# A two-layer trunk with RWKV-7 mixing: triangular blocks inverted by substitution on VectorE for all heads at once, and the chunk chains of two feature tiles taken together

## The chip, the cores and the metric

The kernel runs on one core of one Trainium2 chip. The metric is the device time of one execution in microseconds, as the median of several runs. Times in the trace are microseconds from the first instruction of one profiled execution. PE is TensorE, DVE is VectorE, ACT is ScalarE, POOL is GpSimd and SP is SyncE, which issues most DMAs.

## The reference

One sequence of 256 tokens with 2048 features goes through two layers. Layer 0 mixes tokens by sparse attention with an indexer, layer 1 by RWKV-7; each is followed by a squared-ReLU MLP. The change touches only the scan of layer 1 and the products made for it:

```python
def step(state, inp):
    r_t, k_t, v_t, w_t, kk_t, a_t = inp
    sa = jnp.einsum('bhij,bhj->bhi', state, -kk_t)
    state = (state * w_t[:, :, None, :] + sa[..., None] * (kk_t * a_t)[:, :, None, :]
             + v_t[..., None] * k_t[:, :, None, :])
    return state, jnp.einsum('bhij,bhj->bhi', state, r_t)
_, o = lax.scan(step, state0, (seq_first(rh), seq_first(kh), seq_first(vh),
                               seq_first(dh), seq_first(kk), seq_first(ah)))
```

There are 32 heads of 64 features. The kernel takes the scan in chunks of 64 tokens. Inside a chunk the values that the state is updated with solve a unit triangular system of 64 unknowns, so each chunk of each head needs the inverse of a 64x64 unit triangular matrix: 32 heads x 4 chunks = 128 such systems.

## The kernel before

Activations lie with features on the partitions: 16 feature tiles of 128 features (two heads each) by 256 tokens. Weights come from HBM as pieces of 128x512 (`raw`, six buffers), and each is split into a high part `whi` by ScalarE (L92) and a low part `wlo` by VectorE or, for the pieces named in the phase's `g`, by GpSimd (L94). A dense unit is 16 columns of three matmuls (L184 to L186) of 256 tokens, 48 in all. The phases are `dsa`, `mlp0`, `project`, `scan` and `mlp1`. A planner orders each engine's instructions from the order in the program, priorities (`high_priority(URGENT)` puts work forward) and its own costs of instructions; it also places the semaphore waits.

In `project`, `elements(f)` makes for each tile f the operands of the chunks, `ar` and `bk`, and writes them to HBM (`hd`). Value weights belong to `scan`, but the value of tile 0 is made at the end of `project`.

In `scan`, `prepare(f)` loads the operands of a tile, makes its value (`value`, one dense unit) and the masked products `at` of `bk` and `ar` (L921, L922), transposes `bk` and the value, and makes `akv`. `inverse(f)` inverts the systems of a tile. It takes 32x32 diagonal blocks, begins with their pairs of rows, and doubles the size of what is inverted in four levels; a level is 16 matmuls of 32x32 at L977, a predicated copy on VectorE (L979), 16 matmuls at L984, a transpose on VectorE (L986) and a copy on ScalarE (L989). Then two blocks are merged into one of 64 (L997, L1004). `chain(f)` goes through the four chunks: the state's part (L1032), a sum on VectorE (L1034), the inverse applied (L1037), a copy by ScalarE (L1038), the output (L1040, copied at L1042) and the new state (L1049, L1051, L1058). `finish(f)` normalises and gates the result. When tiles 3, 7, 11, 13 and 15 are done, the output projection `b_w_o` of their block is put in a list in groups, and from tile 5 on one group is taken per tile. The loop over f emits `chain(f)` and `inverse(f+2)` at high priority, then `prepare(f+3)` and `finish(f)`. The phase `scan` has 23 buffers of 128x512 (`A`) and 13 of 128x256 (`B`).

Of the kernel before, what the change touches and what calls it, by code (L numbers as in the profile page):

```python
# [43 lines left out]
AHEAD, AHEAD_INV = 3, 2  # L44
# [19 lines left out]
for _n, _w in (("ident", 128), ("blockones", 128), ("headcol", 2), ("ones", 2), ("mask_a", 256),  # L64
               ("reset", 256), ("pair", 32), ("lvl", 128), ("i32", 32), ("half", 4)):
    CST[_n] = (_at, _w)
    _at += _w
# [34 lines left out]
class Trunk:  # L102
# [587 lines left out]
    def rwkv_project(s, keep):  # L690
# [28 lines left out]
        s.hd = [[s.dram.tile([P, 512], F32, name=f"hd{i}_{f}") for i in range(3)] for f in range(NF)]  # L719
        cols = [k * P for k in range(16)]  # L720
# [52 lines left out]
    def rwkv_scan(s):  # L773
        todo, om, pre = [], [], []
        for f in range(AHEAD):
            pre.append(s.prepare(f))
            if not f:
                s.pairs()
            if f < AHEAD_INV:
                s.inverse(f, pre[f])  # L780
        for f in range(NF):
            cur = pre.pop(0)
            with s.tc.high_priority(URGENT):
                s.chain(f, cur)
            if f + AHEAD_INV < NF:
                with s.tc.high_priority(URGENT):
                    s.inverse(f + AHEAD_INV, pre[AHEAD_INV - 1])
            if f + AHEAD < NF:
                pre.append(s.prepare(f + AHEAD))
            om.append(s.finish(f, cur))  # L790
            if todo and f >= LATE:
                todo.pop(0)()
            if f in CUTS:
                todo += [lambda b=f // 4, o=om, g=g, n=f % 4 + 1 - len(om): s.out_group("b_w_o", 1, b, g, o, n)
                         for g in range(4)]
                om = []
        for t in todo:
            t()

    def pairs(s):  # L800

        nc = s.nc
        i32 = s.cv("i32").unsqueeze(1).to_broadcast([P, 4, 32])
        s.z1, s.yl, s.zf, s.sbd, s.at_sbd = [], [], [], [], 0
        for i in range(3):
            z = s.tp.tile([P, P], F32, name=f"sbd{i}")
            nc.vector.memset(z, 0.0)
            s.sbd.append(z)
        for i in range(2):
            z = s.tp.tile([P, 4, 32], F32, name=f"z1_{i}")  # L810
            nc.scalar.copy(z, i32)
            s.z1.append(z)
            ys = []
            for l in range(4):
                y = s.tp.tile([P, 4, 32], F32, name=f"y{l}_{i}")
                nc.scalar.copy(y, i32)
                ys.append(y)
            s.yl.append(ys)
        for i in range(4):
            z = s.tp.tile([P, 4, 64], F32, name=f"zf_{i}")  # L820
            nc.vector.memset(z, 0.0)
            s.zf.append(z)

# [72 lines left out]

    def value(s, f, v):
        w = s.wload(s.io["b_w_v"][f])
        s.nc.scalar.copy(v, s.dense(w, s.xv, [i * P for i in range(16)]))
        return v  # L900

    def prepare(s, f):
# [13 lines left out]
        for h in range(2):  # L916
            hs = slice(h * 64, h * 64 + 64)
            p = s.bank("m")
            for c in range(4):
                cc = slice(c * P, c * P + P)  # L920
                mm(p[:, cc], bk[hs, cc], ar[hs, cc], start=True, stop=True)  # L921
            nc.vector.tensor_tensor(at[h].rearrange("p (c q) x->p c q x", c=2),  # L922
                                    p.rearrange("p (c q x)->p c q x", c=2, q=2), mask, op=OP.mult)
# [9 lines left out]
        uv = s.A().rearrange("p (c x)->p c x", c=4)  # L933
# [13 lines left out]
        akv = s.B()  # L947
        nc.scalar.copy(akv, p[:, :S])
        return dict(ar=ar, bkt=bkt, uv=uv, at=at, g=g, bv=bv, akv=akv)

    def inverse(s, f, d):
# [4 lines left out]
        at, i = d["at"], f % 2  # L956
        rows = [slice(32 * q, 32 * q + 32) for q in range(4)]
        nt = lambda q, u, c0: at[u // 2][rows[q], 2 * (u % 2) + (1 if q < 2 else 0), c0:c0 + 32]
        z1 = s.z1[i]
        pair = s.cv("pair").bitcast(U32)  # L960
        for q in range(4):
            for h in range(2):
                src = at[h][rows[q]].rearrange("p (c e) x->p c e x", e=2)[:, :, 1 if q < 2 else 0, 32 * q:32 * q + 32]
                nc.vector.copy_predicated(z1[rows[q], 2 * h:2 * h + 2, :],
                                          pair[rows[q]].unsqueeze(1).to_broadcast([32, 2, 32]), src)
        blk = lambda t, q, u: t[rows[q], u * 32:(u + 1) * 32]
        flat = lambda t: t.rearrange("p u x->p (u x)")
        tile = lambda: s.tp.tile([P, P], F32, name=f"xz{i}", bufs=4)
        z, x = flat(z1), tile()
        nc.vector.transpose(x, z)  # L970
        zf = s.zf[f % 4]
        for l in range(4):
            y = s.yl[i][l]
            p = s.bank("ij"[i])
            for u in range(4):
                for q in range(4):
                    mm(blk(p, q, u), nt(q, u, 32 * q), blk(x, q, u), start=True, stop=True)  # L977
            lvl = s.cv("lvl")[:, l * 32:(l + 1) * 32].bitcast(U32).unsqueeze(1).to_broadcast([P, 4, 32])
            nc.vector.copy_predicated(y, lvl, p[:, :P].rearrange("p (u x)->p u x", u=4))  # L979
            y = flat(y)  # L980
            p = s.bank("ij"[i])
            for u in range(4):
                for q in range(4):
                    mm(blk(p, q, u), blk(y, q, u), blk(z, q, u), start=True, stop=True)  # L984
            x = tile()
            nc.vector.transpose(x, p[:, :P])  # L986
            if l < 3:
                z = tile()
                nc.scalar.copy(z, p[:, :P])  # L989
        for q in range(4):  # L990
            o = 32 * (q % 2)
            (nc.scalar.copy if q % 2 else nc.vector.tensor_copy)(zf[rows[q], :, o:o + 32], p[rows[q], :P].rearrange("p (u x)->p u x", u=4))

        p = s.bank("ij"[i])
# [3 lines left out]
        yo = tile()  # L998
        for q in (1, 3):
            nc.scalar.copy(yo[rows[q]], p[rows[q], :P])  # L1000
        p = s.bank("ij"[i])
# [7 lines left out]
    def behind(s, ins, prev):  # L1009
# [3 lines left out]
                            reason="sums in one bank")  # L1013

    def chain(s, f, d):

        nc = s.nc
        ar, bkt, uv, at, zf, akv = (d[k] for k in ("ar", "bkt", "uv", "at", "zf", "akv"))
        mm = nc.tensor.matmul
        d["o"] = ot = s.tp.tile([P, S], F32, name="ot", bufs=2)  # L1020
        st = None
        hs = [slice(0, 64), slice(64, 128)]
        for c in range(4):
# [4 lines left out]
            p = s.bank("ab"[f % 2])  # L1028
            if st is None:
                rs = akv[:, g]  # L1030
            else:
                mm(p[:, :P], ar[:, cc], st, start=True, stop=True)  # L1032
                rs = s.tp.tile([P, P], F32, name="rs", bufs=2)
                nc.vector.tensor_tensor(rs[pu], p[pu, :P], akv[pu, g], op=OP.add)  # L1034
            pd, pn = p[:, P:2 * P], p[:, 2 * P:3 * P]
            for h in range(2):
                mm(pd[pu, hs[h]], zf[pu, 2 * h + c // 2, :], rs[pu, hs[h]], start=True, stop=True)  # L1037
            nc.scalar.copy(uv[pu, c, :], pd[pu])  # L1038
            for h in range(2):
                last = mm(p[pv, hs[h]], at[h][:, c, xr:xr + 64], uv[:, c, hs[h]], start=st is None, stop=True,  # L1040
                          skip_group_check=st is not None)
            nc.scalar.copy(ot[pv, g], p[pv, :P])  # L1042
            if c < 3:
                pc = s.pc[:, f, c:c + 1]
                new = s.sbd[s.at_sbd % 3]
                s.at_sbd += 1
                if st is not None:
                    dec = s.tp.tile([P, P], F32, name="sd", bufs=2)
                    nc.vector.tensor_scalar(dec, st, pc, None, op0=OP.mult)  # L1049
                for h in range(2):  # L1050
                    s.behind(mm(pn[hs[h], hs[h]], bkt[:, c * P + h * 64:c * P + h * 64 + 64], uv[:, c, hs[h]],  # L1051
                                start=True, stop=True), last)
                for h in range(2):
                    o, i, k = new[hs[h], hs[h]], pn[hs[h], hs[h]], pc[hs[h]]
                    if st is None:
                        nc.vector.tensor_scalar(o, i, k, None, op0=OP.mult)
                    else:
                        nc.vector.scalar_tensor_tensor(o, i, k, dec[hs[h], hs[h]], op0=OP.mult, op1=OP.add)  # L1058
                st = new

    def finish(s, f, d):
# [4 lines left out]
        B = lambda: s.tp.tile([P, S], F32, name="fin", bufs=FIN)  # L1066
# [18 lines left out]
        return s.split(w, t=s.O() if f // 4 % 2 else s.tp.tile([P, 512], F32R, name="om", bufs=OM))  # L1085
# [12 lines left out]
def build(tc, io):  # L1098
    with ExitStack() as ctx:
# [27 lines left out]
def constants():  # L1127
# [13 lines left out]
    c["pair"][:] = (j % 2 == 1) & (i == j - 1)  # L1141
    for l, b in enumerate((2, 4, 8, 16)):
        c["lvl"][:, l * 32:(l + 1) * 32] = ((i // b) % 2 == 1) & (j // b == i // b - 1)
# [109 lines left out]
```

## Time and profile before

| | |
|---|---|
| time, median of 3 runs | 2794.97 us (2776.96 to 2795.97) |
| the profiled execution | 2790.62 us |
| its span, first to last instruction | 2788.7 us |
| mean granted TensorE clock | 0.963 |
| instructions | 64443 |
| PE, DVE, ACT, POOL busy | 94%, 70%, 47%, 48% of the span |

The rest of the text counts times in the span. Busy shares are means over stages with different limits; matmuls are pipelined and their ends are modelled, so a busy PE is not PE at its peak.

### The profile page before, as it was taken

How to read it: one execution, taken by the hardware profiler on the slowest of the kernel's cores; microseconds unless marked ns; L12 is line 12 of the kernel's file. 1: busy time of each engine (PE TensorE's matmuls, PEld its weight loads, DVE VectorE, ACT ScalarE, POOL GpSimd, SP SyncE). 2: the span in 40 equal slices, each digit the busy share in tenths (PEclk: the TensorE clock that was granted, in tenths of full speed). 3: DMA queues.
4: the chain of work that ended last, by engine and by line, in shares of the span. 5: the costliest groups of instructions: out<-in, count | busy, mean ns of one | idle time of the engine just before them, and what ended most of it. 6: DMA issues, size and time to landing. Idle time of an engine off the chain costs nothing. (4 is left out here: it accounts for less than half of the span.)

```text
span 2788.7 us, 64443 instructions
## 1 busy us (share of the span) xinstructions
PE 2630.8 (94%) x24884; PEld 2446.9 (88%) x24884; DVE 1957.3 (70%) x3183; ACT 1309.4 (47%) x2852; POOL 1345.3 (48%) x1121
## 2 busy tenths in 40 slices
PE   6898998999999999988889999999899999999998
PEld 4566778999999999888888888888799999999998
DVE  2266568998999999968787655666688377473553
ACT  3334435445444444446555343444455455454553
POOL 1243327566577576655655411233465445444444
PEclk9899999999999999999999887999999999999999
DMA  9997745889899898855557522343467767555553
GB/s 370 393 339 270 255 135 187 312 308 348 283 338 328 286 347 311 302 167 152 172 181 246 173 83 75 89 117 97 146 225 219 222 213 243 183 182 184 182 183 115
DMA packets 263620, 624.73 MB, mean 224 GB/s; under 512 B 29328, under 2 KB 43024, under 8 KB 238352
## 3 DMA queue, kind: packets, MB, share of 16 engines
q1 hardware_dynamic: 256400, 608.03, 65.2%
q10 hardware_dynamic: 6912, 12.59, 1.2%
q8 instruction: 195, 3.19, 0.5%
q14 instruction: 113, 0.93, 0.1%
HBM read 603.72 MB, written 16.78 MB: 222 GB/s over the span
## 5 line engine op out<-in xcount | busy, mean ns | idle before, releaser
L94 POOL TENSOR_TENSOR wlo<-raw,whi 128x512 fp32r<-128x512 f32 x364 | 587.1, 1622 | 544.5 <-ACT whi L92 417.2
L92 ACT CAST whi<-raw 128x512 fp32r<-128x512 f32 x856 | 513.0, 619 | 404.7 <-PE ps_d L185 149.1
L94 DVE TENSOR_TENSOR wlo<-raw,whi 128x512 fp32r<-128x512 f32 x492 | 436.5, 892 | 222.6 <-ACT whi L92 211.0
L94 POOL TENSOR_TENSOR wlo<-more,whi 128x512 fp32r<-128x512 f32 x181 | 263.7, 1460 | 322.7 <-ACT whi L92 165.6
L224 DVE CUSTOM_DVE_ANT_0 araw<-araw,cb 128x2048 f32<-128x2048 f32 x124 | 342.6, 2776 | 4.6 <-DMA araw<-ada_w_in 4.6
L184 PE MATMUL ps_d<-A,whi 128*128 128x256 f32 x1058 | 309.4, 293 | 10.6 <-ACT B L863 6.2
L92 ACT CAST whi<-more 128x512 fp32r<-128x512 f32 x366 | 222.0, 618 | 199.0 <-PE ps_d L185 48.5
L185 PE MATMUL ps_d<-A,whi 128*128 128x256 f32 x1058 | 303.5, 287 | 2.3 <-DVE A L198 2.2
L186 PE MATMUL ps_d<-A,wlo 128*128 128x256 f32 x1058 | 303.1, 287 | 0.5 <-DVE wlo L94 0.5
L94 DVE TENSOR_TENSOR wlo<-more,whi 128x512 fp32r<-128x512 f32 (+1 forms) x185 | 174.3, 943 | 138.8 <-ACT whi L92 135.6
L184 PEld LDWEIGHTS ps_d<-A,whi 128*128 128x128 f32 x1058 | 205.4, 195 | 26.2 <-ACT B L863 7.2
L185 PEld LDWEIGHTS ps_d<-A,whi 128*128 128x128 f32 x1058 | 205.5, 194 | 4.8 <-DVE A L198 3.8
L186 PEld LDWEIGHTS ps_d<-A,wlo 128*128 128x128 f32 x1058 | 205.5, 194 | 1.5 <-DVE wlo L94 0.7
L375 ACT ACTIVATE B<-B,sm 128x256 f32<-128x256 f32 x128 | 65.3, 510 | 247.5 <-DVE B L374 247.4
L185 PE MATMUL ps_d<-h,whi 128*128 128x258 f32 x552 | 157.5, 285 | 3.7 <-DVE h L356 3.7
L186 PE MATMUL ps_d<-h,wlo 128*128 128x258 f32 x552 | 155.8, 282 | 2.5 <-DVE wlo L94 2.4
L184 PE MATMUL ps_d<-h,whi 128*128 128x258 f32 x552 | 156.7, 284 | 0.0
L184 PE MATMUL ps_m<-h,whi 128*128 128x258 f32 x540 | 153.4, 284 | 0.0
L185 PE MATMUL ps_m<-h,whi 128*128 128x258 f32 x540 | 153.1, 284 | 0.0
L186 PE MATMUL ps_m<-h,wlo 128*128 128x258 f32 x540 | 152.1, 282 | 0.0
L376 DVE TENSOR_TENSOR B<-B 128x256 f32<-128x256 f32 x128 | 111.5, 871 | 52.9 <-ACT B L375 52.9
L184 PE MATMUL ps_m<-A,whi 128*128 128x256 f32 x506 | 145.1, 287 | 1.1 <-ACT whi L92 1.1
(552 smaller groups left out, 8773.8 us busy)
## 6 DMA issues: line engine op xcount, KB each, us to landing
araw<-ada_w_in SPq DMA_DIRECT2D x192, 1024.0 KB, 7.2
raw<-mlp_w_in SPq DMA_DIRECT2D x614, 256.0 KB, 4.6
more<-mlp_w_in SPq DMA_DIRECT2D x410, 256.0 KB, 4.1
raw<-b_w_r_in SPq DMA_DIRECT2D x64, 256.0 KB, 3.6
raw<-b_w_k_in SPq DMA_DIRECT2D x64, 256.0 KB, 3.8
raw<-b_w_v_in SPq DMA_DIRECT2D x64, 256.0 KB, 3.6
raw<-b_w_o_in SPq DMA_DIRECT2D x64, 256.0 KB, 3.5
hd<-A ACTq DMA_DIRECT2D x48, 256.0 KB, 4.3
```

Source lines behind the costliest of these rows:

```text
L92: t.nc.scalar.copy(hi[:, :n], r)
L94: e.tensor_tensor(lo[:, :n], r, hi[:, :n].bitcast(F32), op=OP.subtract)
L184: mm(out, wh, m[:, :w], start=i == 0, stop=False)
L185: mm(out, wh, m[:, w:], start=False, stop=False)
L186: mm(out, wl, m[:, :w], start=False, stop=i == n - 1)
L224: nc.vector.tensor_tensor_reduce(out=w, in0=w, in1=s.cb, scale=1.0, scalar=0.0, op0=OP.mult, op1=OP.add, accum_out=acc[:, k:k + 1])
L375: nc.scalar.activation(r, u, AF.Relu, bias=c)
L376: nc.vector.tensor_tensor(q, r, r, op=OP.mult)
```

## The change

The 32x32 diagonal blocks are no longer inverted tile by tile with matmuls. `elements(f)` now also makes the strict triangular products of its tile and writes them to HBM (`nd`), one system to a row of 64x64. At the scan's start `blocks` loads the two diagonal blocks of all 128 systems with one system on each partition, inverts them in 30 steps of three VectorE instructions, and writes the inverses, and for the first block their transposes, to HBM (`xd`). `inverse(f)` loads its blocks from there (six DMAs on SP) and only merges two blocks into one. The values of tiles 1 to 7 are made ahead of the scan, with the low parts of all their weight pieces on GpSimd. `prepare` takes the products of the two halves of the rows in turn, in two PSUM banks. `chain` handles two tiles: the matmuls are those of before, each VectorE and ScalarE step is one instruction for both; the state's decay is multiplied in after the sum. The planner's loop goes by pairs, and `A` and `B` have 19 and 12 buffers.

```diff
-AHEAD, AHEAD_INV = 3, 2
+EARLY_V = 8
...
     def rwkv_scan(s):
...
+        for f in range(1, EARLY_V):
+            s.vs[f] = s.value(f, s.tp.tile([P, S], F32, name="v", bufs=EARLY_V - 1))
+        with s.tc.tile_pool(name="inv", bufs=1, reuse_waits="tile") as ip:
+            s.blocks(ip)
+        with s.tc.tile_pool(name="late", bufs=1, reuse_waits="tile") as s.lp:
+            s.scan()
+
+    def scan(s):
+        todo, om = [], []
+        s.pairs()
+        nxt = s.prepare_pair(0)
+        for f0 in range(0, NF, 2):
+            cur = nxt
             with s.tc.high_priority(URGENT):
...
+                s.chain(f0, cur)
+            if f0 + 2 < NF:
+                nxt = s.prepare_pair(f0 + 2)
+            for i in range(2):
+                f = f0 + i
+                om.append(s.finish(f, cur[i]))
...
+    def prepare_pair(s, f):
...
+        with s.tc.high_priority(URGENT):
+            for i in range(2):
+                s.inverse(f + i, out[i])
+        return out
+
...
+    def blocks(s, ip):
...
+        xt = ip.tile([P, 2, 32, 32], F32, name="xt")
+        for b in range(2):
+            r = slice(b * 32, b * 32 + 32)
+            (nc.sync, nc.scalar)[b].dma_start(xt[:, b], s.nd.rearrange("p (s t) -> p s t", s=64)[:, r, r])
+        nc.vector.memset(xt.rearrange("p b j i -> p b (j i)")[:, :, 0:1024:33], 1.0)
+
+        for j in range(1, 31):
+            i = 31 - j
+            p = s.A()[:, :2 * j * i].rearrange("p (b c i) -> p b c i", b=2, c=j)
+            o = xt[:, :, :j, j + 1:]
+            for b in range(2):
+                nc.vector.tensor_tensor(p[:, b], xt[:, b, j:j + 1, j + 1:].to_broadcast([P, j, i]),
+                                        xt[:, b, :j, j:j + 1].to_broadcast([P, j, i]), op=OP.mult)
+            nc.vector.tensor_tensor(o, o, p, op=OP.add)
+        x = ip.tile([P, 32, 32], F32, name="xn")
+        nc.vector.tensor_copy(x, xt[:, 0].rearrange("p c i -> p i c"))
+        nc.sync.dma_start(s.xd[0], xt.rearrange("p b j i -> p (b j i)"))
+        nc.scalar.dma_start(s.xd[1], x.rearrange("p i c -> p (i c)"))
 
     def elements(s, f, pk, omka, wa0):
 
@@ -894,12 +927,27 @@
...
+        pn = s.bank("c")[:, :S]
+        for c in range(4):
+            x = c * P + (0 if c % 2 else 64)
+            for h in range(2):
+                hs = slice(h * 64, h * 64 + 64)
+                mm(pn[hs, c * 64:c * 64 + 64], bk[hs, x:x + 64], ar[hs, x:x + 64], start=True, stop=True)
+        n = s.B()
...
+        for h in range(2):
+            nc.sync.dma_start(s.nd[f * 8 + h * 4:f * 8 + h * 4 + 4].rearrange("c (s t) -> s c t", s=64),
+                              n[h * 64:h * 64 + 64].rearrange("p (c t) -> p c t", c=4))
+
     def value(s, f, v):
+        g, s.bufs["g"] = s.bufs["g"], (0, 1, 2, 3) if f < EARLY_V else s.bufs["g"]
...
     def prepare(s, f, uv, akv):
...
+        ph = [s.bank("m") for _ in range(2)]
+        for c in range(4):
+            cc = slice(c * P, c * P + P)
+            for h in range(2):
+                hs = slice(h * 64, h * 64 + 64)
+                mm(ph[h][:, cc], bk[hs, cc], ar[hs, cc], start=True, stop=True)
...
     def inverse(s, f, d):
...
         for q in range(4):
...
+            odd, b = 1 if q < 2 else 0, q % 2
+            nc.sync.dma_start(zf[rows[q], :, b * 32:b * 32 + 32], mine[0][odd, b])
+            if not b:
+                nc.sync.dma_start(x[rows[q]].rearrange("p (u c) -> p u c", u=4), mine[1][odd, b])
...
+    def chain(s, f, ds):
...
+            p = s.bank("ab"[f // 2 % 2])
...
+                r = s.lp.tile([P, 2, P], F32, name="rs", bufs=2)
+                nc.vector.tensor_tensor(r[pu], two(p[pu, :S]), akv[pu, :, g], op=OP.add)
...
+            nc.scalar.copy(uv[pu, :, c, :], two(pd[pu]))
...
+            nc.scalar.copy(ot[pv, :, g], two(p[pv, :S]))
...
+                        nc.vector.tensor_tensor(o, i, st[hs[h], :, hs[h]], op=OP.add)
                 if st is not None:
...
+                    nc.vector.tensor_tensor(new, new, pc.to_broadcast([P, 2, P]), op=OP.mult)
                 st = new
...
-            with t.phase("scan", a=23, b=13, m=0, g=(1, 2)):
+            with t.phase("scan", a=19, b=12, m=0, g=(1, 2)):
```

## Rows read from the trace of the kernel before

**Rows 1.** The page, part 1: busy time of each engine over the span.
```profile
PE 2630.8 (94%) x24884; PEld 2446.9 (88%) x24884; DVE 1957.3 (70%) x3183; ACT 1309.4 (47%) x2852; POOL 1345.3 (48%) x1121
```
**Rows 2.** Windows of 50 us: PE, PEld, DVE, ACT, POOL busy, PEclk, DMA share, GB/s.
```profile
1500.00:1550.00 50.00, 46.93 (x396) 44.81 (x395) 40.46 (x73) 27.95 (x68) 35.11 (x61) 1.00 0.74 228
...
1800.00:1850.00 50.00, 50.00 (x904) 44.00 (x904) 33.91 (x93) 23.72 (x62) 16.37 (x14) 1.00 0.37 111
```
**Rows 3.** Windows of 10 us, the same columns.
```profile
1570.00:1580.00 10.00, 6.63 (x34) 5.02 (x36) 4.39 (x13) 1.32 (x3) 0.00 (x0) 0.54 0.68 229
1580.00:1590.00 10.00, 9.84 (x134) 8.14 (x131) 3.53 (x10) 1.53 (x4) 0.00 (x0) 0.50 0.01 2
...
1700.00:1710.00 10.00, 10.00 (x108) 7.97 (x110) 4.96 (x15) 2.18 (x6) 0.00 (x0) 0.50 0.16 33
```
**Rows 4.** Timeline, end of the elements: start, duration, what.
```profile
1562.84 1.51 DVE L892 SCALAR_TENSOR_TENSOR A<-B 128x256 f32<-128x256 f32 x1
```
**Rows 5.** Line 1037: durations in ns min/median/max, first and last start.
```profile
L1037 PE MATMUL ps_a<-B,zf x32: 218/218/365, 1617.7 to 1953.4; 64*64 64x64 f32 x32
```
**Rows 6.** Line 1042, the same columns.
```profile
L1042 ACT COPY ot<-ps_b x32: 248/261/263, 1635.7 to 2005.3; 64x128 f32<-64x128 f32 x32
```
**Rows 7.** Timeline of PE at the scan's start; in brackets the idle time before.
```profile
1563.61 0.28 PE L184 MATMUL ps_d<-xv,whi 128*128 128x256 f32 x1
...
1563.73 0.28 PE L185 MATMUL ps_d<-xv,whi 128*128 128x256 f32 x1
...
1567.09 0.28 PE L186 MATMUL ps_d<-xv,wlo 128*128 128x256 f32 x1
...
1572.92 1.22 PE L910 MATMUL ps_m<-B,cst 128*128 128x256 f32 x2 [5.55 <-DMA B<-hd]
```
**Rows 8.** Windows of line 977 alone: PE busy, PEclk, DMA share, GB/s.
```profile
1860.00:1990.00 130.00, 9.84 (x494) 1.00 0.35 102
```
**Rows 9.** Windows of line 984 alone.
```profile
1860.00:1990.00 130.00, 9.11 (x512) 1.00 0.35 102
```
**Rows 10.** Windows of line 921 alone.
```profile
1860.00:1990.00 130.00, 7.98 (x48) 1.00 0.35 102
```
**Rows 11.** Windows of line 946 alone.
```profile
1860.00:1990.00 130.00, 2.92 (x64) 1.00 0.35 102
```
**Rows 12.** Windows of line 1037 alone.
```profile
1860.00:1990.00 130.00, 9.04 (x80) 1.00 0.35 102
```
**Rows 13.** Timeline of DVE among the elements.
```profile
1457.91 0.41 DVE L890 TENSOR_TENSOR A<-B,A 128x256 f32<-128x256 f32 x1
1458.24 0.41 DVE L892 SCALAR_TENSOR_TENSOR A<-B 128x256 f32<-128x256 f32 x1
1458.58 0.68 DVE L94 TENSOR_TENSOR wlo<-raw,whi 128x512 fp32r<-128x512 f32 x1
1459.18 1.23 DVE L94 TENSOR_TENSOR llo<-raw,lhi 128x512 fp32r<-128x512 f32 x1
```
**Rows 14.** Timeline of POOL in the same stretch.
```profile
1453.12 0.73 POOL L867 TENSOR_TENSOR B<-B 128x256 f32<-128x256 f32 x1
...
1458.86 0.99 POOL L867 TENSOR_TENSOR B<-B 128x256 f32<-128x256 f32 x1
```
**Rows 15.** Line 94: durations in ns min/median/max, first and last start.
```profile
L94 POOL TENSOR_TENSOR wlo<-raw,whi x364: 1265/1302/3438, 25.1 to 2754.4; 128x512 fp32r<-128x512 f32 x182
```
**Rows 16.** DMA queues (packets, MB, share) and issues (count, KB, us to landing).
```profile
q10 hardware_dynamic: 6912, 12.59, 1.2%
...
araw<-ada_w_in SPq DMA_DIRECT2D x192, 1024.0 KB, 7.2
...
rd<-B SPq DMA_DIRECT2D x16, 128.0 KB, 2.9
```
**Rows 17.** Line 907, DMA issues: durations in ns min/median/max, first and last start.
```profile
L907 SPq DMA_DIRECT2D A<-hd x32: 327/424/1271, 1566.6 to 1906.5; - x32
L907 SPq DMA_DIRECT2D B<-hd x32: 319/376/1032, 1568.2 to 1917.7; - x32
```

More of the change, by code (lines that the diff above doesn't have):

```diff
@@ L797, in rwkv_scan @@
         for t in todo:
             t()
+    def prepare_pair(s, f):
+        uv = s.tp.tile([P, 2, 4, P], F32, name="uv", bufs=2)
+        akv = s.tp.tile([P, 2, S], F32, name="akv", bufs=2)
+        ot = s.lp.tile([P, 2, S], F32, name="ot", bufs=2)
+        out = []
+        for i in range(2):
+            d = s.prepare(f + i, uv[:, i], akv[:, i])
+            d.update(o=ot[:, i], pair=(uv, akv, ot))
+            out.append(d)
+        with s.tc.high_priority(URGENT):
+            for i in range(2):
+                s.inverse(f + i, out[i])
+        return out
@@ L966, in inverse @@
         blk = lambda t, q, u: t[rows[q], u * 32:(u + 1) * 32]
[L967 to L994, printed above, removed]
+        p = s.bank("i")
         for u in range(4):
@@ L1013, in behind @@
                             reason="sums in one bank")
-    def chain(s, f, d):
+        return ins
+    def chain(s, f, ds):
         nc = s.nc
-        ar, bkt, uv, at, zf, akv = (d[k] for k in ("ar", "bkt", "uv", "at", "zf", "akv"))
+        uv, akv, ot = ds[0]["pair"]
         mm = nc.tensor.matmul
-        d["o"] = ot = s.tp.tile([P, S], F32, name="ot", bufs=2)
         st = None
         hs = [slice(0, 64), slice(64, 128)]
+        two = lambda t: t.rearrange("p (i x) -> p i x", i=2)
         for c in range(4):
@@ L1027, in chain @@
             cc = slice(c * P, c * P + P)
-            p = s.bank("ab"[f % 2])
+            p = s.bank("ab"[f // 2 % 2])
             if st is None:
-                rs = akv[:, g]
+                rs = [akv[:, i, g] for i in range(2)]
             else:
[L1032 to L1035, printed above, removed]
@@ new lines, in chain @@
+                one, other = (mm(p[:, i * P:i * P + P], d["ar"][:, cc], st[:, i], start=not i, stop=True,
+                                 skip_group_check=i > 0) for i, d in enumerate(ds))
+                s.behind(other, one)
+                r = s.lp.tile([P, 2, P], F32, name="rs", bufs=2)
+                nc.vector.tensor_tensor(r[pu], two(p[pu, :S]), akv[pu, :, g], op=OP.add)
+                rs = [r[:, i] for i in range(2)]
+            pd = p[:, S:]
+            for h in range(2):
+                for i, d in enumerate(ds):
+                    mm(pd[pu, i * P + h * 64:i * P + h * 64 + 64], d["zf"][pu, 2 * h + c // 2, :], rs[i][pu, hs[h]],
+                       start=True, stop=True)
@@ new lines, in chain @@
+            nc.scalar.copy(uv[pu, :, c, :], two(pd[pu]))
+            for i, d in enumerate(ds):
+                for h in range(2):
+                    last = mm(p[pv, i * P + h * 64:i * P + h * 64 + 64], d["at"][h][:, c, xr:xr + 64],
+                              uv[:, i, c, hs[h]], start=st is None, stop=True, skip_group_check=st is not None)
+            if c < 3:
+                pn = two(s.bank("j")[:, :S])
+                for i, d in enumerate(ds):
+                    for h in range(2):
+                        last = s.behind(mm(pn[hs[h], i, hs[h]], d["bkt"][:, c * P + h * 64:c * P + h * 64 + 64],
+                                           uv[:, i, c, hs[h]], start=True, stop=True), last)
```

114 lines of the change are left out of this document (34 added, 80 removed).

## The prediction

> **What bounds the kernel now.** I read the engine shares first: TensorE is busy 94% of the span, and no other engine is near [rows 1]. The windows of the span then say where that holds in the stretch that the change touches. While the RWKV-7 elements are made (1500 to 1550), PE is busy 46.9 of 50 us and VectorE 40.5; in the middle of the scan (1800 to 1850) PE is busy all 50, VectorE 33.9, ScalarE 23.7, GpSimd 16.4 [rows 2]. So a step taken from VectorE or ScalarE in the scan is worth nothing by itself; a matmul taken from PE is worth its place in PE's queue. The reader should see one exception: at the scan's start PE waits for its first loads and runs at 0.54 and 0.50 of its full clock, and it is back at 0.50 from 1700 to 1710 [rows 3]; these are stretches at the lower of its two levels, 1.2 GHz. The scan begins when the last elements are done (the write of `bk`, 1562.84 + 1.51 = 1564.4 [rows 4]), its first chain at 1617.7 [rows 5], and its last chain's copy starts at 2005.3 [rows 6]. From the last dense matmul ahead of PE's wait (1567.1 [rows 7]) that is 438 us.
>
> **Removed: the doubling.** Each feature tile has four levels, each with a group at L977 and one at L984 of 16 matmuls of 32x32, shown as 32 records because f32 takes two: 256 records a tile, 4096 in all. From 1860 to 1990, at full clock, L977 takes 9.84 us for 494 records and L984 9.11 for 512 [rows 8, 9], 19.9 and 17.8 ns each, so 128 x 37.7 ns = 4.8 us a tile and 77 us over 16. This is the upper bound, since the shown end of a matmul overlaps the next: single dense matmuls show 0.28 us but start 0.12 apart [rows 7]. Eight groups a tile each hiding a tail of 0.19 us leave 3.3 us, 53 us in all. I take **60**. The VectorE and ScalarE steps of the levels go too, at no gain.
>
> **Moved: the products of `bk` and `ar`** (L921), 16 records a tile, now alternate between the two halves of the rows and have a bank each. L921 takes 7.98 us for 48, 166 ns each [rows 10], 2.7 us a tile, 43 us in all. L946 also uses two row halves in turn and costs 2.92/64 = 46 ns; L1037, of the same 64x64 shape but in one half, 9.04/80 = 113 ns [rows 11, 12]. By that ratio 25 us go, at worst none; I take **17**, as L946 is nearest but smaller.
>
> **Pairs of tiles.** A chain step of two tiles has one VectorE or ScalarE instruction on twice the columns; the matmuls stay. On engines with room this is 0, in either direction up to 5. The new decay multiply stands after the sum, where `sd` was ahead of it: about 0.4 us more in each of three chunks of a pair. With PE fully booked it is covered; without cover, 8 x 3 x 0.4 = 10 us.
>
> **Added to the elements:** eight 64x64 matmuls a tile (16 records), a masked multiply from PSUM and two stores. PE is busy 94% there, so little of it hides: 16 x 16 x 46 ns = 12 us by L946, 29 by L1037. The halves alternate, so I take the first and a little for the changes of tile shape: **14**. VectorE has 9.5 of 50 us left for 16 multiplies of some 0.41 us (that of a 128x256 operation [rows 13]), 7 us in all. The stores stand on SP's queue behind the multiply, with the weight loads queued after them; those have six buffers, so I cost the wait at 0 (up to 5 if a load comes late).
>
> **Added: the substitution.** Thirty steps j have two products of j(31-j) elements and one sum of twice that: 4960 elements in each product in all, so 19,840 elements in 90 instructions. A 128x256 operation takes 0.41 us and a 128x512 one 0.68 [rows 13], so 1.05 ns an element and 0.14 us fixed: 20.9 + 12.7 = 33.6 us; the second product of a step overlaps the first by 0.07 (0.34 from start to start [rows 13]), so 31 to 34, 0.37 a step, alone. It isn't alone: a VectorE 128x512 difference that begins at 1459.18 takes 1.23 us in place of 0.68 while GpSimd's multiply, 0.99 in place of 0.73, runs [rows 13, 14]. The two take turns. GpSimd's splits of a 128x512 piece take 1.30 us by their median, up to 3.4 [rows 15], and seven values have 28 of them. Where both run, I cost a piece and a VectorE step of 0.37 as 1.67 together.
>
> The Trainium skill, "SBUF — State Buffer", section "SBUF: two separate sides", has the rule behind this: VectorE with two SBUF inputs and GpSimd hold a shared port pair by an exclusive lock for a whole instruction. The row agrees (1.41 us alone against 1.55 for both). By the rule in the extreme, one step for each piece, the overlap would be paid in full, which is how the next sum is made.
>
> **When the first chain starts.** The last elements end at 1564.4 + 14, the new product and its store (a 128 KB store lands in 2.9 [rows 16]) at some 1582. The load of the blocks moves 1 MB in 8192 rows of 128 bytes, 512 for each of 16 engines. No row shows such small pieces. Bounds: by bytes, as the 1 MB loads, 7.2 us; by rows at the mean of the ScalarE queue's packets (1.2% of 16 x 2788.7 us over 6912, 77 ns), 40 us [rows 16]. I take 18, nearer the bytes since those packets are fourteen times as long (12.59 MB over 6912). The Trainium skill's "DMA: Bandwidth & Descriptors", section "Specifications", names 512 bytes as the least size for full rate; by it the load would lie toward the upper bound and the chain start up to 22 us later, which is part of the second rival. So the substitution begins at 1600. Values began at 1580 at 48 x 0.12 = 5.8 us each; some 14 pieces are left to GpSimd, 14 x 1.67 = 23 us, in which VectorE does 14 to 25 steps; the other 65 to 75 take 0.37 each, 26 us, ending at 1649. Then a transposed copy (1.1), a 1 MB store (7), twelve loads issued at 0.38 to 0.42 [rows 17] and landing in 3 to 4 (9 together), and the last merge (3): the chain starts at about **1668**, against 1617.7.
>
> What PE has until then: seven values, 42 us, to 1622 or a little more, and the preparation of four tiles at some 3 us (of the 23 `A` and 13 `B` buffers 19 and 12 remain, at 5 and 3 a tile), to about 1637. So **30 us idle**, less the 6 us wait at the old start [rows 7]. Then the first three pairs have neither values (made already) nor output projections (from tile 5 on) between their steps: a chunk is five engine handovers and some 4.5 us, a pair 18; two pairs can overlap, and with some 16 us of PE work in each I put another **12 us idle**. I leave the half-clock stretches at their old loss: they move to this start. Against that, dense matmuls after a group of small ones start 0.2 us apart instead of 0.12; with 4096 small records fewer, I estimate **10 us** back from 31 dense units of 48.
>
> **Sum**, on the profiled execution (2790.6, span 2788.7): -60 - 17 - 10 + 14 + (30 - 6) + 12 = -37, so 2754; the median of the runs shown is 4.4 us above that execution, so **2758**.
>
> **Rivals.**
> (a) The substitution is hidden: small-row loads go by bytes (-11), GpSimd's splits leave VectorE most slots (-12), and two pairs overlap from the start (-12). Then PE stays booked and the time is 2758 - 35 = 2723. For it: GpSimd stood idle from 1570 to 1590 [rows 3], so it has room to begin its splits early. Against: all pieces of a value now go to GpSimd, 4 x 1.30 = 5.2 of 5.8 us.
> (b) On the other side: the way from the elements to the first chain is the bound. If the load takes 40 us instead of 18 and store and loads twice their 16, that is +38, and a PE at half clock in the bare first pairs adds some 15: 2758 + 53 = 2811. It decides once the first chain starts later than 1668 + 37 = 1705. For it: PE's clock fell after a wait of 5.55 us [rows 3, 7], and every tile waits for one substitution where before each waited only for its own blocks. Against: the byte bound.
> (c) The change doesn't give what its matmuls promise: places freed on PE are filled by waits for the chain, whose chunks now serve two tiles by longer steps (+10), with L921 no faster (+17) and small records near their lower price (+7): 2792, no change.
>
> **Chances.** The forecast with its own range of 2735 to 2780 has 0.48, (a) 0.22, (b) 0.18, (c) 0.12. Measurement tells about 1%, 28 us, from no change. Faster: all of (a) and three quarters of the forecast, 0.58; within 1%: (c), a quarter of the forecast and a little of (b), 0.26; slower 0.16. The range runs from 2705, where (a) meets the 77 us bound of the matmuls, to 2808 near (b).
>
> **What would show it.** In the changed profile: no small matmuls from the levels; L921's successor at about half; a run of 90 VectorE instructions from about 1600 lasting 45 to 55 us, its products stretched only while GpSimd splits; PE idle and at its lower clock before the first chain at 1660 to 1675; the last chain's copy near 1968. I am wrong if the load of the blocks takes over 30 us, if the first three pairs take over 22 us each, or if PE is booked throughout.

## The result, and the profile after

The changed kernel takes 2817.22 us (median, 2814.57 to 2825.09), the kernel before on the same chip 2793.91: a ratio of 1.0102, 95% interval 1.0057 to 1.0146. It is slower by 1.0%, some 28 us by the means of the runs and 23 by the medians; I had forecast 37 less, and a range that ends at 2808. The profiled execution took 2825.09 us, the most of its four runs.

The first two lines are from the page of the changed kernel: the engine shares and the granted clock in 40 slices. The third is the clock of the kernel before.

```profile
PE 2587.4 (92%) x21044; PEld 2417.5 (86%) x21044; DVE 1889.2 (67%) x2881; ACT 1281.8 (45%) x2698; POOL 1345.4 (48%) x1139
...
PEclk9899999999999999999988885799999999999999
...
PEclk9899999999999999999999887999999999999999
```

PE has 3840 records fewer than in [rows 1] (4096 small ones gone, 256 added) and is busy 43 us less in a span that is 35 us longer. So PE waits more. The clock row says where to look: slices 21 to 26 (of 70.6 us each), 1412 to 1835 us, where before only 23 to 25 fell; that is the making of the elements and the start of the scan.

Next come the steps by line, with durations in ns (min/median/max) and first and last start: the write of `bk` (L925), the load of the blocks (L841, and its time to landing), the two lines of the substitution (L849, L851), the loads of a tile's operands (L955), the first chain (L1066), the last copy of the chains (L1079).

```profile
L925 DVE SCALAR_TENSOR_TENSOR A<-B x16: 411/418/419, 1423.1 to 1652.3; 128x256 f32<-128x256 f32 x16
...
L841 SPq DMA_DIRECT2D xt<-nd x1: 390/390/390, 1657.5 to 1657.5; - x1
...
DMA to landing us min/median/max: 9.4/9.8/10.2
...
L849 DVE TENSOR_TENSOR A<-xt x60: 158/368/1469, 1666.9 to 1714.0; 128x30 f32<-128x30 f32 x4, 128x58 f32<-128x58 f32 x4, 128x84 f32<-128x84 f32 x4, 128x108 f32<-128x108 f32 x4
...
L851 DVE TENSOR_TENSOR xt<-xt,A x30: 220/584/1442, 1667.9 to 1714.2; 128x60 f32<-128x60 f32 x2, 128x116 f32<-128x116 f32 x2, 128x168 f32<-128x168 f32 x2, 128x216 f32<-128x216 f32 x2
...
L955 SPq DMA_DIRECT2D A<-hd x32: 381/430/568, 1701.4 to 1972.0; - x32
...
L1066 PE MATMUL ps_a<-akv,zf x32: 218/289/366, 1727.3 to 1958.2; 64*64 64x64 f32 x32
...
L1079 ACT COPY ot<-ps_b x16: 366/366/368, 1767.5 to 2030.0; 64x256 f32<-64x256 f32 x16
```

Three differences against before say where the time went. The elements end at 1652.3 + 0.4 = 1652.7, where they ended at 1564.4 [rows 4]: **88 us later**. From there to the last chain's copy it is 377 us, where it was 441 to [rows 6]: **64 us less**. After that copy it is 793 us against 783, **10 us more**. Together they are the 35 us of the span. The loss lies wholly among the elements, the stretch that I had costed at 14 us. The 16 writes of `bk` show it as a period: (1652.3 - 1423.1)/15 = 15.3 us a tile. In the kernel before, the same line L892 ran from 1429.4 to 1562.8 (the last of them is [rows 4]), 8.9 us a tile:

```profile
L892 DVE SCALAR_TENSOR_TENSOR A<-B x16: 409/416/1514, 1429.4 to 1562.8; 128x256 f32<-128x256 f32 x16
```

The windows of the changed kernel (PE, PEld, DVE, ACT, POOL busy, PEclk, DMA share, GB/s):

```profile
1500.00:1550.00 50.00, 36.92 (x280) 34.19 (x279) 25.57 (x49) 19.18 (x43) 17.17 (x34) 0.84 0.53 164
...
1690.00:1700.00 10.00, 0.00 (x0) 0.00 (x0) 9.76 (x20) 1.51 (x3) 1.72 (x1) 0.50 0.62 200
...
1680.00:1740.00 60.00, 18.20 (x174) 14.65 (x175) 37.85 (x87) 6.67 (x17) 3.89 (x3) 0.57 0.31 100
```

Against [rows 2], every engine is less busy from 1500 to 1550: PE 36.9 for 46.9, VectorE 25.6 for 40.5, GpSimd 17.2 for 35.1. Nothing has taken PE's place as the bound; the engines wait for one another. The waits of the stretch say how (engine, line, what it waited for: us in total, times, longest). First the changed kernel, 1400 to 1650:

```profile
POOL B L878 <- ACT B L877: 77.4, 15, 7.1
ACT whi L92 <- PE ps_d L185: 75.5, 58, 3.0
```

and the same two waits of the kernel before, 1400 to 1560:

```profile
POOL B L845 <- ACT B L844: 29.7, 7, 6.2
...
ACT whi L92 <- PE ps_d L185: 9.5, 9, 2.0
```

L877 is the Tanh at the head of a tile's elements (L844 before). GpSimd now waits for it once in each of 15 tiles, and ScalarE's splits of the next weights wait for PE 58 times in place of 9. The timeline at the end of one tile shows the order, first VectorE, then ScalarE (start, duration, what; in brackets the idle time before):

```profile
1590.67 0.42 DVE L925 SCALAR_TENSOR_TENSOR A<-B 128x256 f32<-128x256 f32 x1
1591.95 0.42 DVE L937 TENSOR_TENSOR B<-ps_a,cst 128x256 f32<-128x256 f32 x1 [0.86 <-PE ps_a L935]
1592.68 0.87 DVE L887 TENSOR_TENSOR_SCAN B<-cst,B 128x256 f32<-128x256 f32 x1 [0.31 <-POOL B L878]
```

```profile
1590.83 0.81 ACTq L928 DMA_DIRECT2D hd<-A  x2
1591.68 0.84 ACT L877 ACTIVATE B<-ps_m,wa 128x256 f32<-128x256 f32 x2 [2.51 <-DVE A L925]
```

The reader should see one tile end and the next begin with nothing between them: the write of `bk`, its stores, then the masked product `n` (L937) and the next tile's two Tanhs within 0.7 us of each other, and after them that tile's scan. The Tanhs don't wait for the multiply itself, since at 1591.68 they start before it; the trace puts the wait there down to the write of `bk`. In all 15 cases the next Tanhs start 1.0 to 2.8 us after that write. In the kernel before, the two Tanhs of each of three tiles start ahead of the write of `bk` at 1515.57:

```profile
1499.53 0.84 ACT L844 ACTIVATE B<-ps_m,wa 128x256 f32<-128x256 f32 x2 [0.94 <-PE ps_a L186]
...
1504.63 0.82 ACT L844 ACTIVATE B<-ps_m,wa 128x256 f32<-128x256 f32 x2
...
1509.28 0.82 ACT L844 ACTIVATE B<-ps_m,wa 128x256 f32<-128x256 f32 x2
```

```profile
1515.57 0.41 DVE L892 SCALAR_TENSOR_TENSOR A<-B 128x256 f32<-128x256 f32 x1
```

About three tiles were under way at once. In the changed kernel the tiles' elements no longer overlap.

**Theory 1.** The overlap is lost because `n` is a `B` buffer. The planner deals out the buffers of one name in the program's order; `n` is the last `B` of a tile and is given its place only once that tile's products are done, so the next tile's first `B` buffers, for the load of `rd` and the outputs of the Tanhs, are given out behind it. **Rival 1:** there are too few `B` buffers. **Rival 2:** the added work itself (matmuls, multiply, stores on SP) costs that much.

### The profile page after: what moved, and what is told of

Its sections match the earlier page's. It is cut to its first block, busy times and chain, and to the rows that moved or that the text cites. A ratio compares the mean times of both kernels' runs of the same rounds, so it can differ in the third digit from the quotient of the medians.

```text
span 2823.3 us, 56523 instructions
## 1 busy us (share of the span) xinstructions
PE 2587.4 (92%) x21044; PEld 2417.5 (86%) x21044; DVE 1889.2 (67%) x2881; ACT 1281.8 (45%) x2698; POOL 1345.4 (48%) x1139
## 4 chain that ended last, share of the span: by engine, by line
PE 40%; DVE 4%; DMA 2%; ACT 2%; issue 1%; POOL 1%; ACTq 0%; SPq 0%; POOLq 0%; DVEq 0%
PE ps_d L184 6%; PE ps_d L185 5%; PE ps_d L186 5%; PE ps_m L184 3%; PE ps_m L185 3%; PE ps_m L186 3%; PE ps_b L185 1%; PE ps_b L184 1%; PE ps_b L186 1%; PE ps_a L184 1%; PE ps_a L185 1%; PE ps_a L186 1%; PE ps_m L969 1%; DMA raw<-b_lora_in 1%; DVE A L849 1%
## 5 line engine op out<-in xcount | busy, mean ns | idle before, releaser
L94 POOL TENSOR_TENSOR wlo<-raw,whi 128x512 fp32r<-128x512 f32 x382 | 604.0, 1591 | 528.1 <-ACT whi L92 369.3
L94 DVE TENSOR_TENSOR wlo<-raw,whi 128x512 fp32r<-128x512 f32 x474 | 422.9, 897 | 235.5 <-ACT whi L92 226.9
L224 DVE CUSTOM_DVE_ANT_0 araw<-araw,cb 128x2048 f32<-128x2048 f32 x124 | 332.0, 2690 | 4.5 <-DMA araw<-ada_w_in 4.4
L184 PE MATMUL ps_d<-A,whi 128*128 128x256 f32 x1058 | 319.9, 303 | 16.4 <-ACT B L896 11.9
L185 PE MATMUL ps_d<-A,whi 128*128 128x256 f32 x1058 | 313.3, 296 | 2.4 <-DVE A L198 2.2
L186 PE MATMUL ps_d<-A,wlo 128*128 128x256 f32 x1058 | 310.2, 293 | 0.4 <-DVE wlo L94 0.4
L184 PEld LDWEIGHTS ps_d<-A,whi 128*128 128x128 f32 x1058 | 214.9, 203 | 34.1 <-ACT B L896 15.2
L185 PEld LDWEIGHTS ps_d<-A,whi 128*128 128x128 f32 x1058 | 215.1, 203 | 5.7 <-DVE A L198 4.7
L186 PEld LDWEIGHTS ps_d<-A,wlo 128*128 128x128 f32 x1058 | 214.5, 203 | 0.7 <-DVE wlo L94 0.6
```

What stands on the lines that cost most here:

```text
L94: e.tensor_tensor(lo[:, :n], r, hi[:, :n].bitcast(F32), op=OP.subtract)
L184: mm(out, wh, m[:, :w], start=i == 0, stop=False)
L185: mm(out, wh, m[:, w:], start=False, stop=False)
L186: mm(out, wl, m[:, :w], start=False, stop=i == n - 1)
L224: nc.vector.tensor_tensor_reduce(out=w, in0=w, in1=s.cb, scale=1.0, scalar=0.0, op0=OP.mult, op1=OP.add, accum_out=acc[:, k:k + 1])
```

## The experiments

Edits are to the changed kernel unless said otherwise. The kernel before was timed on the same chips, at 2780 to 2784 us.

**`n` in buffers of its own name.**

```diff
-        n = s.B()
+        n = s.tp.tile([P, S], F32, name="nt", bufs=2)
```

> The changed kernel with one edit: the masked products `n` of `elements` get two buffers of their own instead of one of the 16 `B`. Theory 1 (the planner hands out the buffers of one name in the order of the program; `n` is the last thing of a tile, so the next tile's `B` tiles wait for it and the tiles no longer overlap): the last elements end near 1575 instead of 1652.8, the tiles follow each other every 9 to 10 us instead of 15.3, and the time falls from 2817 to about 2740. Theory 2 (16 buffers are too few for two tiles of nine): the same fall here, and again with 18 `B`. Theory 3 (PE's queue waits at the new matmuls, or SP's queue at the new stores): nothing changes, 2805 to 2820, since both stay.

Measured: 2738.18 us, ratio 0.9843 (0.9822 to 0.9865). That one line is worth 72 us (1.0102 - 0.9843 = 2.59% of 2781), and with it the change makes the kernel faster. The same lines as above, of this kernel:

```profile
L925 DVE SCALAR_TENSOR_TENSOR A<-B x16: 410/417/1507, 1421.3 to 1567.8; 128x256 f32<-128x256 f32 x16
...
L955 SPq DMA_DIRECT2D A<-hd x32: 369/430/1148, 1620.2 to 1887.0; - x32
...
L1066 PE MATMUL ps_a<-akv,zf x32: 218/289/366, 1646.1 to 1873.2; 64*64 64x64 f32 x32
...
L1079 ACT COPY ot<-ps_b x16: 366/367/369, 1684.7 to 1945.0; 64x256 f32<-64x256 f32 x16
```

The period is back at (1567.8 - 1421.3)/15 = 9.8 us, with all the added work still there. So are the shares of the engines among the elements, PE again at the 46.9 us of [rows 2]:

```profile
1500.00:1550.00 50.00, 46.90 (x433) 43.79 (x432) 39.83 (x69) 26.34 (x62) 37.26 (x56) 1.00 0.68 217
```

**Two more `B` buffers in that phase.**

```diff
-            with t.phase("project", a=21, b=16, l=3, m=0):
+            with t.phase("project", a=21, b=18, l=3, m=0):
```

> The changed kernel with 18 `B` buffers in `project` instead of 16, and `n` among them. Theory 1 (order of the program): no change, 2817 within 15, elements still 15 us a tile. Theory 2 (their number): near 2740, as with buffers of its own. Theory 3 (waits in PE's or SP's queue): no change.

Measured: 2818.79 us, ratio 1.0135 (1.0101 to 1.0168), the time of the changed kernel. Its write of `bk`:

```profile
L925 DVE SCALAR_TENSOR_TENSOR A<-B x16: 410/416/419, 1419.8 to 1647.6; 128x256 f32<-128x256 f32 x16
```

Still 15.2 us a tile. The buffers are 18 in all, as in the first experiment (16 and 2), and only the name differs: rival 1 falls. Many more `B` buffers, or `n` taken from `B` at another place in the program, were not tried.

**The added products alone, in the kernel before.** Its `elements` gets the eight matmuls, the multiply into `s.B()` and the two stores; what they write is read by nobody.

```diff
+        pn = s.bank("c")[:, :S]
...
+                mm(pn[hs, c * 64:c * 64 + 64], bk[hs, x:x + 64], ar[hs, x:x + 64], start=True, stop=True)
+        n = s.B()
...
+            nc.sync.dma_start(s.nd[f * 8 + h * 4:f * 8 + h * 4 + 4].rearrange("c (s t) -> s c t", s=64),
```

> The kernel before with the added products of `elements` alone: eight matmuls, the masked multiply into a `B` buffer and two stores a tile, whose result nothing reads. Theory 1 (order of the program in `B`): the tiles follow each other every 15 us instead of 8.9 and the time rises by 80 to 95 us, to about 2870. The prediction's own term: 14 us more, 2800.

Measured: 2872.67 us, ratio 1.0321 (1.028 to 1.0362), 89 us for the added part with nothing else changed. Its write of `bk` (L893), 15.2 us a tile:

```profile
L893 DVE SCALAR_TENSOR_TENSOR A<-B x16: 416/416/419, 1425.7 to 1653.5; 128x256 f32<-128x256 f32 x16
```

**The same, with `n` in its own name.** The edit of the first experiment on top of this one.

> The kernel before with the added products, multiply and stores, their result unread, but the multiply into two buffers of a name of its own instead of a B buffer. Theory (the B buffer ends the overlap of the tiles' elements): the added work by itself is the small term of the prediction, so 5 to 15 us over the kernel before (ratio 1.002 to 1.006), tiles' elements following every 9 to 10 us, and the rest of the +89 of the same edit with a B buffer is the buffer. Rival (the matmuls, the multiply and the stores cost by themselves): still 40 us or more, ratio above 1.014, whatever name the buffer has.

Measured: 2790.72 us, ratio 1.0029 (1.0008 to 1.005), and 9.2 us a tile.

```profile
L893 DVE SCALAR_TENSOR_TENSOR A<-B x16: 410/418/1506, 1433.6 to 1571.6; 128x256 f32<-128x256 f32 x16
```

So the work itself costs 8 us and the buffer's name 81 (3.21% less 0.29%): rival 2 falls, and the buffer taken from `B` is shown to be the cause. That the planner deals buffers out in the program's order is the reading that fits these four runs and the order in the timelines; the runs show the name and the lost overlap, not the planner's inside.

**The products of the substitution in buffers of their own.** The first operands of the scan (`A<-hd` above) were loaded 49 us after the elements' end in the changed kernel and 51 in the first experiment (1569.3 to 1620.2). They are `A` buffers, and the program asks for the thirty products of the substitution, `A` buffers too, ahead of them. This kernel has the edit to `n` as well, as have all that follow on the changed kernel.

```diff
-            p = s.A()[:, :2 * j * i].rearrange("p (b c i) -> p b c i", b=2, c=j)
+            p = ip.tile([P, 512], F32, name="pt", bufs=2)[:, :2 * j * i].rearrange("p (b c i) -> p b c i", b=2, c=j)
```

> The changed kernel with `n` in buffers of its own and, besides, the products of the substitution in two buffers of their own instead of the scan's `A`. By theory 1 the first pair's loads, which come behind 30 products in the order of `A`, are issued near the scan's start instead of 44 us later, and PE does the products and transposes of two to four tiles while VectorE substitutes: 10 to 20 us less than with the first edit alone, about 2725. Rival (VectorE, busy with the substitution, keeps the preparation waiting anyway): within 5 us of the first edit.

Measured: 2726.7 us, ratio 0.9805 (0.9778 to 0.9833), 11 us better than with `n` alone; on the same chip, the slowest of its runs (2730.67) is below the fastest there (2735.73).

```profile
L955 SPq DMA_DIRECT2D A<-hd x32: 370/430/1776, 1579.3 to 1873.2; - x32
...
L1066 PE MATMUL ps_a<-akv,zf x32: 218/289/366, 1649.5 to 1859.4; 64*64 64x64 f32 x32
...
L1079 ACT COPY ot<-ps_b x16: 365/366/368, 1663.9 to 1931.2; 64x256 f32<-64x256 f32 x16
```

The loads go out 41 us earlier and the first pairs are prepared beside the substitution: from 1600 to 1650 PE is busy 32.6 us, where it was 8.6 in the first experiment. The first chain is no earlier, but it has more ready behind it, and the last copy comes 14 us earlier.

The stretched steps of the substitution are plain here. VectorE beside GpSimd at 1588, then a row of VectorE at 1633, when GpSimd has nothing to do:

```profile
1588.10 2.53 DVE L849 TENSOR_TENSOR pt<-xt 128x130 f32<-128x130 f32 x2
1590.66 1.40 DVE L851 TENSOR_TENSOR xt<-xt,pt 128x260 f32<-128x260 f32 x1
...
1632.42 0.50 DVE L849 TENSOR_TENSOR pt<-xt 128x130 f32<-128x130 f32 x2
...
1633.29 0.42 DVE L851 TENSOR_TENSOR xt<-xt,pt 128x260 f32<-128x260 f32 x1
```

```profile
1587.76 5.45 POOL L94 TENSOR_TENSOR wlo<-raw,whi 128x512 fp32r<-128x512 f32 x4 [0.79 <-ACT whi L92]
```

The same two products take 2.53 us and 0.50, the same sum 1.40 and 0.42. The Trainium skill, "SBUF — State Buffer", section "SBUF: two separate sides", gives the rule that GpSimd and a VectorE instruction with two SBUF inputs exclude each other for a whole instruction; these rows agree: each of the three stretched instructions is 1.0 us longer, most of a split's 1.36 (5.45/4).

**Four early values in place of eight.** Fewer splits on GpSimd beside the substitution.

```diff
-EARLY_V = 8
+EARLY_V = 4
```

> The repaired kernel (own buffers for `n` and for the substitution's products, 2727 us) with four values made ahead in place of eight. Theory A (GpSimd's splits hold up the substitution, which took 55 us there against 34 worked out alone): GpSimd is done before the blocks arrive, so the substitution takes 36 to 42 us, the first chain starts some 15 us earlier, and the four later values fill PE between the first pairs: 2700 to 2715. Rival B (what counts is PE's work before the first chain): four units, 24 us, less of it are done in the gap, of which 15 come back: 2730 to 2740.

Measured: 2730.04 us, ratio 0.9816 (0.9787 to 0.9844), no gain over the eight. The windows of the two lines alone (DVE busy, PEclk, DMA share, GB/s) of this kernel, L849 and then L851:

```profile
1560.00:1730.00 170.00, 20.19 (x60) 0.72 0.41 115
...
1560.00:1730.00 170.00, 16.00 (x30) 0.72 0.41 115
```

The substitution's own time is 36.2 us, 8 less than the 44.5 with eight early values (26.50 + 17.97 in the same view), yet it runs from 1587 to 1639 and the first chain starts at 1650, as with eight (1649.5). What fills the rest on VectorE is, by that trace, 7.1 us of the preparation of the pairs (L960, L971), which the earlier loads let in, 4.8 us of splits and some waiting.

**The low parts of early values shared with VectorE,** as the rest of the scan has them.

```diff
-        g, s.bufs["g"] = s.bufs["g"], (0, 1, 2, 3) if f < EARLY_V else s.bufs["g"]
+        g, s.bufs["g"] = s.bufs["g"], s.bufs["g"]
```

> The repaired kernel with the early values' pieces shared as in the rest of the scan: GpSimd takes two of four, VectorE the other two. Theory A (the two engines take turns): GpSimd's 14 pieces fewer shorten the substitution by some 8 us, VectorE's own 14 pieces of 0.69 us cost 10: 2727 within 6. Rival B (GpSimd's rate of 5.2 us a value holds PE back while values are made): 5 to 10 us less.

Measured: 2722.62 us, ratio 0.9789 (0.9758 to 0.9819). It is the fastest version with the change's parts whole, but its interval overlaps that of the own product buffers alone, so this last edit isn't told from nothing.

**Chains of single tiles again.** `chain` in its form before the change, called twice for a pair (on the kernel with both own buffers).

```diff
-                s.chain(f0, cur)
+                for i in range(2):
+                    s.chain(f0 + i, cur[i])
```

> The repaired kernel with the chains of the kernel before, one tile each, two at a time on two PSUM banks: 24 more VectorE and ScalarE steps a pair, the decay multiplied ahead of the sum. The prediction's term for pairs is 0 within 5: 2722 to 2732. Rival: in the stretch after the first chain's start PE waits for handovers; a step for two tiles halves them, so single chains cost 10 to 25 us more.

Measured: 2759.21 us, ratio 0.9911 (0.9886 to 0.9936). Pairing is worth 30 us (0.9911 - 0.9805 = 1.06% of 2784; the intervals don't meet), where I had put 0. The windows of this kernel (columns as above), and its last copy:

```profile
1680.00:1720.00 40.00, 38.37 (x276) 29.68 (x276) 15.80 (x46) 11.85 (x37) 4.93 (x6) 0.50 0.17 45
1720.00:1760.00 40.00, 39.59 (x362) 34.24 (x358) 21.00 (x52) 17.31 (x43) 12.95 (x12) 0.84 0.35 110
...
L1066 ACT COPY ot<-ps_b x32: 258/260/260, 1656.0 to 1968.8; 64x128 f32<-64x128 f32 x32
```

The kernel that pairs, in the same two windows:

```profile
1680.00:1720.00 40.00, 37.09 (x344) 30.55 (x344) 17.50 (x46) 14.09 (x36) 9.06 (x11) 0.69 0.23 66
1720.00:1760.00 40.00, 39.40 (x405) 35.98 (x406) 21.94 (x46) 18.43 (x41) 15.84 (x14) 1.00 0.41 136
```

Both show PE busy nearly all the time, but the pairs finish 749 matmul records in the 80 us and the single chains 638: the lower clock (0.50 and 0.84 against 0.69 and 1.00) lasts longer with single chains. The mean granted clocks of all runs agree (0.955 to 0.963 with pairs, 0.950 to 0.955 without). Part of what pairing gives thus goes with an earlier end of the half-clock stretch; how much of the 30 us that is was not separated. The last copy comes 38 us earlier with pairs (1931.2 against 1968.8), but what follows it is 8 us longer (793 against 785): the pairs give back 8 us at the scan's end. That is most of the 10 us by which the stretch after the last copy is longer in the changed kernel than before (783).

**The alternating products, alone in the kernel before.**

```diff
-        for h in range(2):
-            hs = slice(h * 64, h * 64 + 64)
-            p = s.bank("m")
-            for c in range(4):
+        ph = [s.bank("m") for _ in range(2)]
+        for c in range(4):
...
+            for h in range(2):
```

> The kernel before with one part of the change alone: the products of `bk` and `ar` alternate between the two halves of the rows, with a PSUM bank each. The prediction's term: 17 us less (bounds 0 and 25), so 2777 from 2794; busy time of that line falls from 166 ns a record to 70 to 90. Rival (PE's place is filled by waits): the records are cheaper but the time stays within 5 us.

Measured: 2792.84 us, ratio 1.004 (1.0028 to 1.0052): 11 us slower, where I had 17 saved. Windows of L921 alone (PE busy, PEld busy, PEclk, DMA share, GB/s), and the earlier window of the kernel before, whose later one is [rows 10]:

```profile
1760.00:1860.00 100.00, 8.61 (x64) 6.89 (x64) 1.00 0.34 107
1860.00:1990.00 130.00, 7.50 (x48) 5.78 (x48) 1.00 0.34 102
```

```profile
1760.00:1860.00 100.00, 10.03 (x64) 7.92 (x64) 1.00 0.38 111
```

A record takes 134 and 156 ns, where it took 157 and 166 before. The records are little shorter, and the time doesn't follow even that. Why it is slower, these runs don't tell.

**The old order of these products, in the fastest version.** The same edit backwards.

> The changed kernel with all three repairs (own buffers for the masked products and for the substitution's products, split pieces of early values shared), but the products of bk and ar in the old order, one half of the rows after the other. If the alternation is worth what its records show in the changed kernel (100 ns against 166, 16 records a tile, 256 in all): 17 us more, 2740. If it is worth nothing, as alone in the kernel before: within 6 us of 2723.

Measured: 2720.71 us, ratio 0.9781 (0.9763 to 0.9799), the same as with alternation. Windows of the products' line alone, first with the old order, then with alternation:

```profile
1700.00:1900.00 200.00, 17.62 (x160) 15.32 (x160) 0.98 0.41 131
```

```profile
1700.00:1900.00 200.00, 16.68 (x160) 13.81 (x160) 1.00 0.41 131
```

110 ns a record without alternation, 104 with it. The drop from 166 that I expected of the alternation appears in this kernel without it.

## Why the prediction was wrong

**The step that failed** is the one on what is added to the elements, where eight matmuls, a multiply and two stores a tile were costed by their durations at 14 us. The stretch got 88 us longer. The durations were nearly right: with `n` in its own name the same work costs 8 us in the kernel before. What I left out is the multiply's output buffer: the sum has no term for a wait that it causes. With it taken from `B` each tile starts when the one before it ends, and the overlap of about three tiles was what kept PE busy 46.9 of 50 us [rows 2]; it fell to 36.9, and came back to 46.9 with the buffer's own name. I counted `A` and `B` buffers for the scan, where the change lowers them, and not for the elements, where it adds a user.

**The result is rival (b)'s side, not its mechanism.** The first chain starts at 1727.3, past the 1705 from which (b) decides. But the way from the elements' end to the first chain is 74.6 us (77 in the first experiment), less than the 90 that I had put, 1578 to 1668. It started late because the elements ended late.

**Other terms**, by what the runs gave:
- The load of the blocks: 9.4 and 10.2 us, near its byte bound of 7.2, not 18. My upper bound from the ScalarE queue's packets was far off. The Trainium skill, "DMA: Bandwidth & Descriptors", section "Specifications", asks for 512 bytes at least; at 128 bytes, 1 MB took 1.4 times the 7.2 us of the large loads [rows 16], so the size may cost something here, but little, and not the 22 us of the estimate.
- The substitution: 47.6 us (1666.9 to 1714.5) against 49, and its mechanism, turns between VectorE and GpSimd, is in the rows above. That the length fits so well is partly luck: its own instructions take 42.6 us there (24.55 and 18.02 in the view of the two lines), 9 to 12 more than the 31 to 34 alone, where the turns were to add 15 to 18; other VectorE instructions and gaps make up the rest.
- PE idle, 30 us before the first chain and 12 among the first pairs: from 1680 to 1740 it is busy 18.2 of 60 us, so 41.8 idle. It was at its lower clock there, too (0.50 from 1690 to 1700). But "I leave the half-clock stretches at their old loss" was too simple. The mean clock is 0.54, 0.60 and 0.80 in the three windows of 50 us from 1600 of the first experiment, and 0.80 and 0.85 in the two of 100 us from 1560 of the kernel before; by the two levels, that is an estimated 106 us at half clock against 70.
- The first three pairs, by my count 18 us each, with over 22 as a sign of being wrong: they took 45, 31 and 37 us (from the first matmul of L1066 to the last copy of L1079: 1727.3 to 1772.0, 1753.8 to 1784.8, 1796.4 to 1833.1). The sign came true, but it isn't what made the kernel slower: they take 43, 29 and 39 us in the first experiment, which is faster than the kernel before. The load of the blocks and PE's idle time gave no such sign.
- Pairs, "0, in either direction up to 5": 30 us gained. I argued from engines with room in the middle of the scan; the windows of 1680 to 1760 show part of the gain at its start, which I had not looked at for this term.
- The alternating products, -17: nothing in the fastest version, 11 us lost alone. [rows 11] was no guide to [rows 10].
- The doubling, -60, with -10 for dense starts and +36 for the start of the scan, is -34. With the pairs undone the time is 25 us below that of the kernel before (0.9911); less the 8 us of the added work, that leaves -33 for this group and the alternation together. None of its terms was run by itself, so errors that cancel would not show.

**The sum made again**, against the kernel before: -34 for that group, -30 for pairs, 8 for the added work and 0 for alternation is -56; the version with both own buffers measured -1.95% of 2781, -54. Only the -34 in this is forecast; the others are differences of the runs, and alternation alone gave +11. The change as it stands adds 11 us for the `A` buffers of the substitution and 72 for the `B` buffer of `n`; these too are differences of the runs, so that they lead back to the measured +28 is no further check. So the time came from the parts that I named and from pairing, and two buffer names more than took it back. With them mended the change gains 54 us, between my 37 and the 72 of rival (a), although the substitution isn't hidden as (a) has it: pairing, which (a) didn't price and the sum put at 0, is in it with 30.

## What to carry to other kernels

Where a planner deals out buffers by name, a new temporary is an edge in the order of work: ask which buffer name it takes, when in the unit's life it is filled, and which first instruction of the next unit draws from the same name; a step filled last gets a name of its own. When every engine's share falls in a window and no engine's rises, look for lost overlap of units, by the period of one line that runs once a unit, before costing any instruction. A record's duration prices a matmul only as long as its neighbours stay: shorter records twice brought no time here.

## What the runs showed of the hardware

- A VectorE sum over 260 elements on 128 partitions takes 0.42 us alone and 1.40 beside GpSimd's splits, more than three times as long, though both engines show as busy.
- A load of 512 KB in rows of 128 bytes on each of two queues landed in 9.4 to 10.2 us.
- The lower clock doesn't end when PE is booked again: with single chains PE is busy 38.37 of 40 us from 1680 to 1720 and is granted 0.50 throughout, 1.2 GHz. Before that stretch PE had waited 14.36 us for a VectorE step, up to 1618.5, and the clock was at 0.50 from 1610 on. What ends such a stretch stays open.
- The products of `bk` and `ar`, with the same matmuls in the same order, show 157 and 166 ns a record in two windows of the kernel before and 110 in the version without the doubling. Their shown time isn't a matter of their own form alone; which of the differences between the two kernels shortened it, no run separates.
